# Letting a planner order all five engines of a two-layer diffusion block

## The chip, the cores and the metric

The kernel runs on one core of a Trainium2 chip. A core has five engines that work side by side, each through its own instructions in its own fixed order: TensorE (PE, the matmuls), VectorE (DVE), ScalarE (ACT), GpSimd (POOL) and SyncE (SP, which issues most of the DMAs). An instruction whose input is not there yet holds up everything behind it on its engine. The metric is the device time of one execution in microseconds (us).

## The reference

Two layers work on 256 tokens and 256 context positions of 1024 channels, all in float32. A layer is a half-step FFN, a mixer over four groups of 256 channels, and a second half-step FFN; each is modulated by vectors that a large matrix `ada_w` makes out of a condition vector:

```python
def half_ffn(h, shift, scale, gate, g, wi, wo):
    return h + 0.5 * gate * swiglu(modulate(rms_norm(h, g), shift, scale), wi, wo)
def swiglu(h, wi, wo):
    a, g = jnp.split(h @ wi, 2, axis=-1)       # 1024 -> 2 x 2816
    return (jax.nn.silu(g) * a) @ wo           # 2816 -> 1024
def modulate(h, shift, scale):
    return h * (1 + scale) + shift
```

The mixer's four groups are a pooling, a long convolution with a filter made by a small MLP (hyena), a gated linear attention (GLA) in two directions, and a short convolution. Layer 1's second FFN and the output are needed for the 256 tokens alone.

## The kernel before

**Work.** All activations lie with channels on the 128 partitions and the 512 positions (tokens v = 0, context v = 1) along the free axis. A float32 product is made of three fp32r matmuls (`mm3`, lines 178 to 180): each operand is split into a rounded high part and a low part (`split`: ACT casts `whi`, line 166; DVE subtracts to get `wlo`, line 167). So each weight tile is loaded by DMA (`raw`, 1 MB), cast, subtracted, and multiplied. An up block f of an FFN is 48 matmuls of 128x512 (8 k, two halves, 3 each), and its result goes through Silu (`sg`, lines 500 and 501) and a split (`hh`, `hl`). 22 up blocks and two sweeps of down blocks make an FFN.

**Fp32 matmuls.** Some products stay plain fp32: the statistics of the norm (line 390), the broadcast of their reciprocal root (line 227, `diag`), the modulation vectors of the start (`gemv`, line 280), and the small products of the mixer. The `gemv` ones use a quarter of the array each: `c32` has 32 columns, and step k writes partitions 32(k mod 4) on:

```python
for k in ks:
    g = slice(32 * (k % 4), 32 * (k % 4) + 32)
    self.nc.tensor.matmul(ps[g, :], lhsT=self.c32[:, k, :], rhs=ws[k], start=k < 4, stop=k >= KT - 4)
```

**Modulation.** The other modulation vectors are made on DVE: `acc` (lines 316 and 318) multiplies and adds 128x512 pieces of `ada_w`; transposes (322) and sums (324) follow. This work is cut into small steps by a generator, and `fill` hands out some steps after each FFN block.

**Order.** The framework's scheduler sets the order by priorities in program order. Three tools bend it: `prio` shifts a priority, `mark` and `after` hold an instruction behind one issued earlier, and `start()`, the first two up blocks with the first norm and four slabs of modulation, is issued by hand in written order on PE, DVE and ACT. Its slabs are written as: slab 0 (`part(0)`), first matmuls (lines 1315 to 1318), slab 1, more matmuls, slab 2, and so on, each slab with its 8 `gemv` matmuls in one go. The norm at the start is: squares on ACT (376), sums on DVE (380), line 390 on PE, a chain of 12 small DVE operations (`rsqrt_cols`, 205 to 215), `diag` (225), line 227; then `ny` (421) on DVE, `yh` (428) on ACT, `yl` (429) on DVE.

**GLA.** The mixer computes the logarithm of a decay for both directions (matmul 1080, then ACT: 1082, 1083, a table load, 1086), a scan on DVE (1095), `kexp` (DVE 1106, ACT exponential 1107, DVE 1109), a transposition on PE (1113), and then the states (1151).

## Time and profile before

| | us |
|---|---|
| three runs | 1703.17, 1704.85, 1704.58; median 1704.58 |
| profiled execution | 1703.05 |
| its span, first to last instruction | 1701.3 |
| PE busy | 1672.0 (98%) |
| DVE busy | 1199.1 (70%) |
| ACT busy | 577.8 (34%) |

The stages in the profiled execution, by the first matmul of each: start to 21.1, layer 0 FFN 1 to 408, mixer to 616, FFN 2 to 984, layer 1 FFN 1 to 1358, mixer to 1493, FFN 2 to 1691, output to 1701. A row of a timeline gives the start, the length of the record and the instruction; the records of neighbouring matmuls overlap, so what one costs is the distance from its start to the next one's.

### The profile page before, as it was taken

The page shows a single profiled execution, that of the slowest core. Times are in us where ns is not written, and L with a number is a line of the kernel's source. Part 1 is how long each engine was busy: PE and PEld are TensorE (multiplying, and loading weights), DVE is VectorE, ACT ScalarE, POOL GpSimd, SP SyncE. Part 2 cuts the span into 40 slices and gives each one's busy share as a digit, 9 for nine tenths or more (in the row PEclk, how much of TensorE's full clock was granted, in tenths as well). Part 3 has the DMA queues.
Part 4 walks back from the last instruction along what each step waited for, and adds up shares of the span by engine and source line. Part 5 has one row for each costly group of instructions (what it writes and reads, how often), then busy time and mean ns, then how long its engine had stood idle before and what let it go on. Part 6 is the DMA issues. An engine that isn't in the chain of part 4 may idle for free.

```text
span 1701.3 us, 23406 instructions
## 1 busy us (share of the span) xinstructions
PE 1672.0 (98%) x9590; PEld 1434.0 (84%) x9590; DVE 1199.1 (70%) x2053; ACT 577.8 (34%) x741; POOL 33.6 (2%) x59
## 2 busy tenths in 40 slices
PE   8999999999999999999999999999999998999998
PEld 6888887878888898888888898888878897899998
DVE  5889957896675679888669775654464668875455
ACT  3322213333632443221122242221233354554343
POOL 0000000010000000000000000000000000000010
PEclk9999999999999999999999999999999999999999
DMA  8655544432322325545435425543433234345552
GB/s 331 244 180 190 196 163 164 162 123 98 115 100 93 115 94 184 193 164 176 180 131 203 162 108 176 173 161 137 158 117 118 78 127 161 117 153 174 181 194 78
DMA packets 50875, 262.54 MB, mean 154 GB/s; under 512 B 5946, under 2 KB 10880, under 8 KB 28240
## 3 DMA queue, kind: packets, MB, share of 16 engines
q1 hardware_dynamic: 48672, 255.99, 43.0%
q0 software_dynamic: 1376, 4.00, 0.6%
q8 instruction: 75, 1.23, 0.3%
q10 hardware_dynamic: 720, 1.06, 0.2%
q14 instruction: 32, 0.26, 0.0%
HBM read 257.88 MB, written 3.15 MB: 153 GB/s over the span
## 4 chain that ended last, share of the span: by engine, by line
PE 91%; DVE 5%; ACT 2%; DMA 1%; issue 1%; POOL 0%; DVEq 0%; ACTq 0%; POOLq 0%; SPq 0%
PE psm L178 28%; PE psm L179 27%; PE psm L180 27%; DVE wlo L167 1%; ACT whi L166 1%; DVE acc L318 1%; PE psa L991 1%; PE psm L1315 1%; PE psa L227 1%; DMA x<-in_xt_dram 0%; PE psa L1050 0%; PE psm L1316 0%; PE psa L1228 0%; PE psm L1318 0%; PE psa L390 0%
## 5 line engine op out<-in xcount | busy, mean ns | idle before, releaser
L178 PE MATMUL psm<-yh,whi 128*128 128x512 f32 (+1 forms) x1584 | 555.7, 354 | 4.8 <-ACT yh L428 1.8
L180 PE MATMUL psm<-yh,wlo 128*128 128x512 f32 (+1 forms) x1584 | 556.8, 353 | 2.4 <-DVE wlo L167 2.4
L179 PE MATMUL psm<-yl,whi 128*128 128x512 f32 (+1 forms) x1584 | 556.7, 353 | 0.2 <-DVE yl L429 0.2
L166 ACT CAST whi<-raw 128x2048 fp32r<-128x2048 f32 (+5 forms) x176 | 304.8, 1734 | 596.2 <-PE psm L179 522.2
L167 DVE TENSOR_TENSOR wlo<-raw,whi 128x2048 fp32r<-128x2048 f32 (+5 forms) x176 | 364.3, 2071 | 139.3 <-ACT whi L166 138.9
L178 PEld LDWEIGHTS psm<-yh,whi 128*128 128x128 f32 x1584 | 297.4, 189 | 49.1 <-ACT yh L428 2.3
L180 PEld LDWEIGHTS psm<-yh,wlo 128*128 128x128 f32 x1584 | 299.3, 189 | 44.8 <-DVE wlo L167 3.4
L179 PEld LDWEIGHTS psm<-yl,whi 128*128 128x128 f32 x1584 | 298.9, 189 | 41.2 <-DVE yl L429 0.9
L318 DVE SCALAR_TENSOR_TENSOR acc<-adaw,cvec,acc 128x512 f32<-128x512 f32 x392 | 274.5, 746 | 2.8
L178 PE MATMUL psm<-hh,whi 128*128 128x512 f32 (+1 forms) x752 | 264.7, 352 | 0.0
L180 PE MATMUL psm<-hh,wlo 128*128 128x512 f32 (+1 forms) x752 | 264.6, 352 | 0.0
L179 PE MATMUL psm<-hl,whi 128*128 128x512 f32 (+1 forms) x752 | 264.4, 352 | 0.0
L180 PEld LDWEIGHTS psm<-hh,wlo 128*128 128x128 f32 x752 | 142.3, 189 | 19.3 <-DVE acc L318 0.8
L179 PEld LDWEIGHTS psm<-hl,whi 128*128 128x128 f32 x752 | 142.3, 189 | 19.3 <-DVE hl L167 0.4
L178 PEld LDWEIGHTS psm<-hh,whi 128*128 128x128 f32 x752 | 142.2, 189 | 18.9 <-issue 0.2
L501 DVE TENSOR_TENSOR sg<-psm,sg 128x512 f32<-128x512 f32 (+1 forms) x90 | 54.4, 605 | 127.0 <-PE psm L180 119.8
L484 DVE SCALAR_TENSOR_TENSOR x<-psm,gt,x 128x256 f32<-128x256 f32 x112 | 50.4, 478 | 116.2 <-PE psm L180 116.1
L500 ACT ACTIVATE sg<-psm 128x512 f32<-128x512 f32 (+1 forms) x90 | 47.9, 532 | 208.1 <-PE psm L180 203.6
L376 ACT ACTIVATE sq<-x 128x512 f32<-128x512 f32 (+1 forms) x64 | 32.7, 522 | 91.1 <-DVE x L484 75.1
L178 PE MATMUL psm<-whi,yh 128*128 128x256 f32 (+1 forms) x200 | 58.2, 293 | 1.6 <-ACT whi L166 1.6
L179 PE MATMUL psm<-wlo,yh 128*128 128x256 f32 (+1 forms) x200 | 57.4, 293 | 1.2 <-DVE wlo L167 1.2
L180 PE MATMUL psm<-whi,yl 128*128 128x256 f32 (+1 forms) x200 | 58.0, 290 | 0.0
(291 smaller groups left out, 1515.7 us busy)
## 6 DMA issues: line engine op xcount, KB each, us to landing
raw<-in_ffn_wi_dram SPq DMA_DIRECT2D x86, 1024.0 KB, 4.8
adaw<-in_ada_w_dram SPq DMA_DIRECT2D x68, 1024.0 KB, 5.1
raw<-in_ffn_wo_dram SPq DMA_DIRECT2D x32, 896.0 KB, 4.6
raw<-in_ffn_wo_dram SPq DMA_DIRECT2D x16, 1024.0 KB, 5.0
raw<-in_w_in_dram SPq DMA_DIRECT2D x14, 1024.0 KB, 4.7
raw<-in_w_out_dram SPq DMA_DIRECT2D x8, 1024.0 KB, 4.7
adaw<-in_ada_w_dram SPq DMA_DIRECT2D x16, 256.0 KB, 5.7
pm<-in_k_pool_dram SPq DMA_DIRECT2D x12, 256.0 KB, 2.8
```

The lines of the kernel that those rows point to most:

```text
L166: self.nc.scalar.copy(hi[:, s], src[:, s])
L167: self.nc.vector.tensor_tensor(lo[:, s], src[:, s], hi[:, s].bitcast(F32), op=ALU.subtract)
L178: mm(ps, lhsT=ah, rhs=bh, start=first, stop=False)
L179: mm(ps, lhsT=ah, rhs=bl, start=False, stop=False)
L180: mm(ps, lhsT=al, rhs=bh, start=False, stop=last)
L227: nc.tensor.matmul(ps[:, j * P:(j + 1) * P], lhsT=self.ones, rhs=dg[:, j, :], start=True, stop=True)
L318: nc.vector.scalar_tensor_tensor(acc, ws[half][:, k, :], sc, acc, op0=ALU.mult, op1=ALU.add)
L376: nc.scalar.activation(sq, self.x[m][:, lo:lo + n], AF.Square)
L484: nc.vector.scalar_tensor_tensor(self.x[m][:, s], ps[:, v * S - lo:v * S - lo + S], gate[v][:, m:m + 1], self.x[m][:, s], op0=ALU.mult, op ...
L500: nc.scalar.activation(sg, w[2][:, s], AF.Silu)
L501: nc.vector.tensor_tensor(sg, w[3][:, s], sg, op=ALU.mult)
L991: nc.tensor.matmul(ps[par], lhsT=fwd[:, 2 * i + par, :], rhs=cur[par], start=True, stop=True)
```

## The change

Every call that the builder makes on an engine is written down instead of issued (`_Engine`, `Plan.add`), with what it must follow: earlier calls that touch the same part of the same tile, and, for a tile from a rotating pool, the end of the tile whose place it takes. `cost` gives each call a length. `forward` is a list schedule: the engine that can start first takes the ready call of the lowest rank. `backward` gives latest times. Ten mixtures of early and late times, in two rounds, are tried; the shortest plan is issued in order of its start times, on all five engines. `prio`, `mark` and `after` do nothing any more. The calls themselves are the same.

```diff
+class Plan:
+    def cost(self, eng, op, out, args, kw):
+        if op == "dma_start":
+            return 0.45, 0.0
+        n = self.free(out)
+        if eng == "PE":
+            if op == "transpose":
+                return 0.115, 0.33
+            lhs = kw["lhsT"]
+            m, k = self.free(lhs), lhs.shape[0]
+            if "32r" in str(lhs.dtype):
+                d = max(0.0135 + n / 2400.0, 0.06)
+            else:
+                d = 2 * max(0.112 * min(m, 128) / 128.0, 0.002 + n / 1200.0)
+                if m in (32, 64):
+                    d *= m / 128.0
+                elif k <= 64:
+                    d *= 0.62
+            return d, d + 0.3
+        psum = any(str(a.space).endswith("PSUM") for a in self.aps(args, kw))
+        if eng == "DVE":
+            cyc = {"tensor_tensor_scan": 2.0, "reciprocal": 4.0}.get(op, 1.0)
+            if op == "tensor_reduce":
+                n = self.free(args[1])
+            d = (0.13 if psum else 0.07) + cyc * n / 960.0
+            return d, d + 0.2
+        if eng == "ACT":
+            d = 0.19 + n * 0.8e-3
+            return d, d + 0.2
...
+    def forward(self, rank, queue):
...
+            t, e = best
+            while soon[e] and soon[e][0][0] <= t + 1e-9:
+                r, i = heapq.heappop(soon[e])
+                heapq.heappush(now[e], (rank[i], i))
+            if e == "ACT":
+                _, i = min(now[e], key=lambda x: (x[0] + (2.0 if self.table[x[1]] not in (-1, table) else 0.0), x[1]))
...
+            if e == "ACT" and self.table[i] not in (-1, table):
+                t += 1.3
+                table = self.table[i]
+            start[i] = t
+            order.append(i)
+            clock[e] = t + self.occ[i]
+            if self.bytes[i]:
+                wire = max(wire, t + self.occ[i] + 1.3) + self.bytes[i] / 0.38e6
...
+    def issue(self, tc, rounds=2):
...
+        for _ in range(rounds):
+            start, end = best
+            late = self.backward(start)
+            for early in (start, [i * end / n for i in range(n)]):
+                for share in (0.125, 0.25, 0.375, 0.5, 0.75):
+                    rank = [share * e + (1 - share) * (b + end) for e, b in zip(early, late)]
+                    got = self.forward(rank, self.queue)
+                    if got and got[1] < best[1]:
+                        best = got
+        start = best[0]
+        self.planned = best
+        with tc.manual_schedule():
+            for i in sorted(range(n), key=lambda i: (start[i], i)):
+                fn, args, kw = self.calls[i]
+                fn(*args, **kw)
...
-        self.tc, self.nc, self.t, self.out = tc, tc.nc, t, out
+        self.tc, self.nc, self.t, self.out = tc, Plan(tc.nc), t, out
...
-        with self.tc.manual_schedule(engines={et.PE, et.DVE, et.Activation}):
+        if True:
...
-        Builder(ctx, tc, t, out).run()
+        b = Builder(ctx, tc, t, out)
+        b.run()
+        b.nc.issue(tc)
```

Three places of the new order follow. In it every instruction has the line of the issuing loop (L341), so the names tell them apart; their numbers differ between the two programs.

**ACT at the start.** `x_...` are the eight tiles of the input, `craw` the condition vector, from which Silu makes `cvec`; `sq` are the squares. Before:

```order
L1266 DMA craw_111<-in_cvec_dram 128x16
L370 DMA x_113<-in_xt_dram 128x512
L370 DMA x_115<-in_xt_dram 128x512
L370 DMA x_117<-in_xt_dram 128x512
L370 DMA x_119<-in_xt_dram 128x512
L247 ACT_TABLE_LOAD
L247 ACTIVATE cvec_108<-craw_111 128x16
L376 ACTIVATE sq_228<-x_112 128x512
L376 ACTIVATE sq_230<-x_113 128x512
```

And now, from the fourth `x` on:

```order
L341 DMA x_116<-in_xt_dram 128x512
L341 DMA craw_108<-in_cvec_dram 128x16
L341 ACT_TABLE_LOAD
L341 ACTIVATE sq_146<-x_110 128x512
...
L341 ACTIVATE sq_149<-x_113 128x512
L341 ACTIVATE sq_152<-x_116 128x512
L341 ACT_TABLE_LOAD
L341 ACTIVATE cvec_105<-craw_108 128x16
L341 ACTIVATE sq_151<-x_115 128x512
```

The condition vector is fetched last instead of first, and the Silu with a table load of its own stands between the seventh and the eighth square.

**PE at the start.** `adaw` with `c` is a slab's matmul (line 280); `mean` with `sq` is line 390, `diag` line 227, `psm` the up blocks. Before:

```order
L390 MATMUL psa_251<-mean_102,sq_228 128x2 x4
L280 MATMUL psa_305<-adaw_131,c_41_184 32x512 x4
L280 MATMUL psa_305<-adaw_133,c_41_184 32x512 x4
L227 MATMUL psa_316<-diag_317,ones_100 128x128 x2
L227 MATMUL psa_322<-diag_323,ones_100 128x128 x2
L292 MATMUL psa_330<-sum_22_137,row_314 128x2 x4
L1315 MATMUL psm_295<-yh_277,whi_293 128x512
```

And now, up to the first up matmul, and a piece from slab 3:

```order
L341 MATMUL psa_153<-mean_101,sq_145 128x2 x3
L341 MATMUL psa_191<-adaw_119,c_41_141 32x512 x4
L341 MATMUL psa_191<-adaw_120,c_41_141 32x512 x2
L341 MATMUL psa_153<-mean_101,sq_145 128x2
L341 MATMUL psa_191<-adaw_120,c_41_141 32x512 x2
...
L341 MATMUL psa_202<-adaw_128,c_41_141 32x512
L341 MATMUL psm_181<-yh_163,whi_179 128x512
...
L341 MATMUL psa_212<-adaw_140,c_41_141 32x512
L341 MATMUL psm_181<-yh_165,whi_179 128x512
L341 MATMUL psa_212<-adaw_140,c_41_141 32x512
```

One of the four statistics matmuls stands behind six slab matmuls, six of slab 1's stand ahead of the first up matmul, and the last four of slab 3's stand alone between up matmuls.

**PE in layer 1's GLA.** `kexp` is line 1113, `v` with `kdt` line 1151, `psm` are projections. Before, the two transpositions stand 55 rows apart:

```order
L1113 MATMUL psa_11209<-ident_99,kexp_11205 128x128 x4
L180 MATMUL psm_11443<-whi_11358,yl_10713 128x256
...
L180 MATMUL psm_11524<-yh_10707,wlo_11490 128x256
L1113 MATMUL psa_11233<-ident_99,kexp_11229 128x128 x4
L1151 MATMUL psa_11253<-v_10950,kdt_11214 32x64 x4
```

And now:

```order
L341 MATMUL psm_1964<-whi_1957,yl_1822 128x256
L341 MATMUL psa_1909<-ident_99,kexp_1908 128x128 x4
L341 MATMUL psm_1965<-whi_1960,yh_1807 128x256
L341 MATMUL psa_1916<-ident_99,kexp_1915 128x128 x4
L341 MATMUL psm_1967<-whi_1957,yh_1807 128x256
L341 MATMUL psa_1922<-v_1872,kdt_1910 32x64 x4
```

They are one matmul apart, and the states begin one matmul later.

## Rows read from the trace of the kernel before

**Rows 1.** The page: busy time of each engine; the chain that ended last.

```profile
PE 1672.0 (98%) x9590; PEld 1434.0 (84%) x9590; DVE 1199.1 (70%) x2053; ACT 577.8 (34%) x741; POOL 33.6 (2%) x59
PE 91%; DVE 5%; ACT 2%; DMA 1%; issue 1%; POOL 0%; DVEq 0%; ACTq 0%; POOLq 0%; SPq 0%
```

**Rows 2.** Busy time in stretches: PE, PEld, DVE, ACT, POOL; granted clock; DMA share, GB/s.

```profile
10.00:22.00 12.00, 7.84 (x61) 5.97 (x61) 8.02 (x31) 3.58 (x8) 0.00 (x0) 0.90 1.03 390
22.00:56.00 34.00, 33.62 (x171) 23.22 (x170) 18.40 (x48) 14.49 (x27) 0.00 (x0) 0.93 0.81 309
56.00:400.00 344.00, 342.50 (x1539) 281.63 (x1540) 287.30 (x459) 97.30 (x99) 9.96 (x14) 1.00 0.49 171
100.00:150.00 50.00, 50.00 (x222) 41.40 (x221) 44.43 (x66) 15.03 (x15) 0.00 (x0) 1.00 0.50 172
400.00:425.00 25.00, 21.68 (x162) 19.96 (x161) 19.55 (x62) 10.51 (x24) 1.18 (x3) 1.00 0.20 72
425.00:562.00 137.00, 136.81 (x1026) 113.77 (x1025) 93.09 (x164) 56.07 (x86) 2.10 (x4) 1.00 0.31 106
1355.00:1375.00 20.00, 17.22 (x117) 16.03 (x116) 15.84 (x48) 9.89 (x22) 0.00 (x0) 0.91 0.16 53
1375.00:1493.00 118.00, 110.64 (x967) 100.30 (x966) 94.23 (x205) 62.58 (x108) 1.05 (x2) 1.00 0.41 141
1493.00:1690.00 197.00, 196.28 (x1628) 194.19 (x1627) 111.30 (x138) 84.43 (x98) 7.59 (x8) 1.00 0.47 161
```

**Rows 3.** Timeline of PE at the start: start, length, instruction, idle before.

```profile
13.67 1.02 PE L390 MATMUL psa<-mean,sq 128*128 128x2 f32 x8 [1.56 <-DVE sq L380]
14.63 1.92 PE L280 MATMUL psa<-adaw,c 128*32 128x512 f32 x16
17.25 1.17 PE L227 MATMUL psa<-diag,ones 128*128 128x128 f32 x8 [0.70 <-DVE diag L225]
21.11 0.79 PE L1315 MATMUL psm<-yh,whi 128*128 128x512 f32 x1 [1.91 <-ACT yh L428]
```

**Rows 4.** Timeline of ACT at the start.

```profile
4.04 1.28 ACT L247 ACT_TABLE_LOAD   x1 [4.04 <-DMA craw<-in_cvec_dram]
12.17 0.63 ACT L376 ACTIVATE sq<-x 128x512 f32<-128x512 f32 x1 [2.20 <-DMA x<-in_xt_dram]
```

**Rows 5.** Timeline of PE, eight full-width fp32 matmul records of 512 columns.

```profile
482.29 3.60 PE L991 MATMUL psa<-tok,dft 128*128 128x512 f32 x8
```

**Rows 6.** Groups of DVE instructions, 60 to 350 us: shape, count, busy, mean ns.

```profile
L318 DVE SCALAR_TENSOR_TENSOR acc<-adaw,cvec,acc 128x512 f32<-128x512 f32 x160 | 110.1, 744 | 0.5
L167 DVE TENSOR_TENSOR wlo<-raw,whi 128x2048 fp32r<-128x2048 f32 x18 | 41.2, 2286 | 10.3 <-ACT whi L166 10.3
L322 DVE STREAM_TRANSPOSE acct<-acc 128x256 f32<-128x256 f32 x44 | 16.8, 419 | 0.3
L501 DVE TENSOR_TENSOR sg<-psm,sg 128x512 f32<-128x512 f32 x18 | 12.3, 684 | 7.9 <-PE psm L180 7.9
```

**Rows 7.** Timeline of DVE, a pair of line 318 in one row.

```profile
119.73 1.41 DVE L318 SCALAR_TENSOR_TENSOR acc<-adaw,cvec,acc 128x512 f32<-128x512 f32 x2
```

**Rows 8.** Waits of PE: released by, us in total, times, longest.

```profile
PE psa L227 <- DVE diag L225: 2.2, 5, 0.7
PE psa L1113 <- DVE kexp L1109: 2.1, 2, 1.6
```

**Rows 9.** Timeline of layer 1's GLA: two rows of PE, one of ACT.

```profile
1399.52 0.70 PE L1080 MATMUL psa<-g,gw 96*128 96x512 f32 x2
1411.19 0.66 PE L1113 MATMUL psa<-ident,kexp 128*128 128x128 f32 x4 [1.62 <-DVE kexp L1109]
...
1401.16 1.25 ACT L1082 ACTIVATE la<-psa,vec 128x512 f32<-128x512 f32 x2
```

**Rows 10.** Timeline of PE, a projection matmul and the next state matmul.

```profile
1421.71 0.38 PE L178 MATMUL psm<-yh,whi 128*128 128x256 f32 x1
1422.03 0.70 PE L1151 MATMUL psa<-v,kdt 64*32 64x64 f32 x24
```

More of the change, by code (lines that the diff above doesn't have):

```diff
@@ L1 @@
+import heapq
 import math
@@ L108, in prio @@
     def prio(self, delta):
-        tc = self.tc
-        base = tc.cur_priority
-        tc.cur_priority = max(0, base + delta)
-        start = tc.cur_priority
         yield
-        tc.cur_priority = base + tc.cur_priority - start
     def mark(self, *engines):
-        engines = engines or (mybir.EngineType.DVE, mybir.EngineType.SP)
-        found = {}
-        for i in reversed(self.nc.cur_bb.bb.instructions):
-            if i.engine in engines and i.engine not in found:
-                found[i.engine] = i
-                if len(found) == len(engines):
-                    break
-        return found
+        return None
     @contextmanager
     def after(self, mark):
-        with ExitStack() as es:
-            for i in mark.values():
-                es.enter_context(self.tc.issue_after(i))
-            yield
+        yield
     def consts(self):
@@ L1285, in start @@
         nc.sync.dma_start(out=self.tneg, in_=self.t["k_tneg"])
-        et = mybir.EngineType
         two = [0, 1]
-        with self.tc.manual_schedule(engines={et.PE, et.DVE, et.Activation}):
+        if True:
             self.ada_init(craw)
```

194 lines of the change are left out of this document (added).

## The prediction

> **What bounds the kernel now.** I read the page first. PE is busy 98% of the span and holds 91% of the chain that ended last; DVE is at 70%, ACT at 34% [rows 1]. So an order can win only where PE idles, and it can lose wherever it makes PE's own work longer.
>
> Next the busy time in stretches [rows 2] says where PE idles. From 100 to 150 us it is busy 50.00 of 50 with 222 matmuls, one per 0.225 us: in an FFN there is nothing to win. From 56 to 400 it idles 1.5 of 344 us, from 425 to 562 0.2 of 137, from 1493 to 1690 0.7 of 197. The idle time lies at the start (4.2 of the 12 us from 10 to 22), at the entries of the two mixers (3.3 from 400 to 425, 2.8 from 1355 to 1375) and in layer 1's mixer (7.4 of 118). The granted clock, 1.00 elsewhere, averages 0.90, 0.93 and 0.91 in three of these rows. As its levels are 1.2 and 2.4 GHz, that is 2.4 + 4.8 us at the lower level in the start and 3.6 at the second mixer entry, each time behind a stretch in which PE idled.
>
> Then the timelines of the start [rows 3, 4], of GLA [rows 9] and of a change between matmul forms [rows 10] give the prices.
>
> **Start, step by step.** The planner fetches `craw` last on ACT and puts a table load, 1.28 us [rows 4], ahead of the eighth square, which in the trace starts at 12.17 when its input lands [rows 4]. If the inputs land as late as now, the table load hides in that wait and costs nothing; if not, table load and square push line 390 by up to 1.3 + 0.6 us. I take 0.5, since ACT idled 2.2 us there.
>
> One of the four line-390 matmuls now stands behind six of slab 0's. In the trace line 390 runs at 13.67 and the slab, 1.92 us, at 14.63 [rows 3]. The reciprocal root reads all four columns, so it starts about 1.9 us later. Behind it, `wlo` casts of 512 columns now stand inside the chain on DVE: a cast of 2048 takes 2.29 in the record [rows 6], a quarter of that is 0.6. Before, `yh` was also waited for by PE for 1.91 us at 21.11 [rows 3], so nothing on PE hides this: the sum is 0.5 + 1.9 + 0.6 = 3.0. But before, `ny` also had to wait for the modulation of line 292, which ends behind line 227, so not all of it is new; I take +2.3 (bounds 0.5 and 3.5).
>
> The slabs themselves: 16 records in 1.92 us are two passes of each of 8 matmuls, four column groups side by side, so a round of four takes 0.96 us [rows 3]. A lone one has two passes of 512 columns, and eight such passes took 3.60 us [rows 5], so it takes 0.90, not a quarter of a round. Counted so, slabs 1 to 3 took 6 rounds after the first up matmul. Now slab 1 leaves 2 there (its six stand ahead, in time in which PE waits anyhow), slab 2 takes 2, and slab 3, split 2, 2, 1, 1, 1, 1, takes 6: 10 rounds, +4 x 0.9 = 3.6 us. If a lone matmul cost only an eighth of a slab, 0.24, the term would be 18 x 0.24 less 24 x 0.24 = -1.4; I take 3.6, the nearer row. Nothing hides it: from 22 to 56 PE was busy 33.6 of 34 [rows 2]. As the clock's low stretch will hold fewer up matmuls if they start later, I give back 0.5. Start: **+5.4** (0 to +8).
>
> **First FFN.** The order on DVE packs the `acc` work early. Between two `wlo` casts of up blocks there now stand nine operations of line 318. A pair of them takes 1.41, one record 0.744 [rows 6, 7], so the second starts 0.67 after the first. A cast takes 2.29 less the same 0.07, 2.2; `sg` and `hl` 0.6 each, six transposes and sums up to 0.34 each [rows 6]. That is 6.0 + 2.2 + 1.2 and, in some blocks, 2.0: 9.4 to 11.4, where a block of PE has 48 x 0.225 = 10.8 us. It is even on the average, with two `wlo` buffers as cover. I take **+1** (0 to +4). If the cover were gone, every block with sums would cost 0.6.
>
> **Mixer entries.** Between line 390 and line 227 of the context's half the order before has 15 matmuls, now 43, so the wait for `diag`, 2.2 us over five places [rows 8], and for `yh` behind it goes there. The tokens' half has about as few as before. Of 3.3 + 2.8 idle I take half, and half of what the lower clock cost at the second (3.6 us at half speed lose 1.8): -3.0 - 0.9 = **-3.9** (0 to -7.9). The turns between FFNs hold 1.5 and 0.7 us in their rows [rows 2]; I take **-1** for all of them.
>
> **GLA in layer 1.** From line 1080 at 1399.52 to line 1113 at 1411.19 the chain took 11.7 us, with a PE wait of 1.62 in it [rows 9]. Now 72 matmuls of 256 columns lie between; 1628 in 197 us make 0.12 each [rows 2], so 2 x 0.3 + 72 x 0.12 = 9.2 us of cover. The chain gets another table load, 1.28 [rows 4], and begins up to 0.6 earlier on ACT, which was late at 1401.16 [rows 9]: 12.4, so PE waits 3.2. The second transposition comes a matmul later and waits for its own `kexp`, 0.5; the states follow at once and wait for the copy `kdt` on ACT, which stands behind exponentials, 0.8. That is 4.5 against 2.1 for the two waits now [rows 8]: **+2.4** (-1 to +4). The other 5.3 us of idle in this mixer have more filler than before, projection and output groups dealt out one by one; I take **-4** (0 to -5.3).
>
> **Changes of form.** The planner holds a small fp32 matmul to be as cheap anywhere. From a projection matmul at 1421.71 to the state matmul at 1422.03 it took 0.32 instead of 0.12 [rows 10], so such a visit costs 0.2. Counted in the orders, fp32 work visits the fp32r stream 155 times instead of 99: 7 more at the start, 8 in the FFNs, 41 in the mixers, of which about 20 with tiles smaller than the array. I take 20 x 0.2 less 0.5 that falls into waits: **+3.5** (0, if the change hides, to 56 x 0.2 = 11).
>
> Outside these the matmuls and their lengths are the same, and the last stage has the same chain.
>
> **The sum.** 5.4 + 1 - 3.9 - 1 + 2.4 - 4 + 3.5 = +3.4 on the profiled execution's 1703.05 (span 1701.3 and 1.75 around it); the median of the runs is 1.5 above that execution, so 1704.6 + 3.4 = **1708 us**. Under 0.2%, 3.4 us, a measurement of this kernel can hardly tell from no change; the forecast lies on that edge.
>
> **The rivals.**
>
> *Faster: the plan fills the waits.* What speaks for it is that 13.5 us of idle lie in stretches with other matmuls at hand, and that the planner sees all five engines where the old order saw priorities. If 80% of it goes, with the 1.8 of the clock, and start and form changes cost 5 together, the time falls by 10.8 + 1.8 - 5 = 7.6: **1697**. It decides for this if the wait at line 1113 is under 1 us and the first part of the start costs under 3. Against it: its small DVE operations are planned at 0.07 us plus length, and its chains therefore too short. The Trainium skill, Perfetto Trace Analysis, Optimization Strategy, holds that interleaving stretches in which different engines are contended can gain. Here it does not apply between FFN and mixer as long as PE is full in the one [rows 2].
>
> *Slower: DVE becomes the bound of the first FFN.* Blocks of 11.4 against 10.8 us, once the two buffers' lead is used up, give 0.6 in each of some 17 blocks that carry `acc` work: +10 on top of a balance of nothing else changed by much, **1716**. For it: DVE is busy 287 of 344 us there already [rows 2]. Against it: blocks without sums are 9.4. It decides if PE shows waits for `wlo` between 150 and 350 us.
>
> *Slower: every change of form costs.* If all 56 additional visits cost 0.2, not just those with small tiles, the term is 11.2 instead of 3.5: **1716**. For it is the one row of the price [rows 10]; against it, that full-array fp32 matmuls load and stream like the others. The Trainium skill, TensorEngine Tiling (Array Packing), Tiling Modes, says that a change of the tiling mode drains TensorE. By that rule only the visits with small tiles cost, which gives the forecast's term; the 0.2 us of the trace agree with it.
>
> *The change does nothing* can be left out: the order differs on all engines.
>
> **How the numbers follow.** Forecast 0.45, with its own range of 1701 to 1714; filled waits 0.28; DVE bound 0.13; all form changes 0.14. The forecast splits into 0.06 faster, 0.20 the same and 0.19 slower; the filled waits give 0.27 faster and 0.01 the same; of the two slow rivals 0.04 come out the same. So faster 0.33, same 0.25, slower 0.42. The range leaves out 1 in 10 on each side: 1691, where the filled waits meet a start near its lower bound, to 1718, just past the slow rivals.
>
> **What the profile after would show.** First up matmul near 23.4 instead of 21.1, the lone slab matmuls 0.9 apart from what follows, end of the first two blocks some 5 us later; no new PE waits for `wlo` at 100 to 350 us; shorter idle at the mixer entries and no low clock at the second; a wait of about 3 us at line 1113; 0.3 instead of 0.12 around small-tile visits. Wrong would be the forecast if lone slab matmuls take 0.24, if PE's idle time in layer 1's mixer falls under 3 us, or if waits for `wlo` repeat block after block.

## The result, and the profile after

The changed kernel takes 1767.47 us, median of 4 runs (1766.51 to 1770.54), against 1703.88 (1702.84 to 1704.85) for the kernel before on the same chip. The ratio is 1.0376, with a 95% interval of 1.0358 to 1.0394: 64 us slower, where 1708 and at most 1718 had been forecast.

The page of the kernel after: busy time of each engine, the chain that ended last by engine; below them the answer on the core, with the mean granted clock. Every instruction has the line of the issuing loop, so only engines and names speak.

```profile
PE 1708.9 (97%) x9590; PEld 1448.6 (82%) x9590; DVE 1224.7 (69%) x2053; ACT 580.9 (33%) x744; POOL 32.9 (2%) x59
PE 48%; DVE 21%; issue 2%; ACT 1%; DMA 1%; SPq 0%; DVEq 0%; ACTq 0%
...
core 0: 1765.9 us, clock 0.986
```

DVE's part of the chain has gone from 5% to 21% [rows 1], though its busy share is a point lower. These shares add up to 74%: the chain could be followed back to 456 us only, so the first FFN and the first mixer's entry are not in it. The span is 64.6 us longer. PE idles 1765.9 - 1708.9 = 57.0 us instead of 29.3: +27.7. The mean clock was 0.996 before and is 0.986 now, so 0.014 x 1765.9 = 24.7 us of work were lost to the lower level instead of 0.004 x 1701.3 = 6.8: +17.9. The other 19 us PE was busy longer without idling or the lower clock, on the same matmuls.

By stage, each counted from the first statistics matmul of its norm to that of the next stage's:

| stage | before | after | |
|---|---|---|---|
| start and layer 0 FFN 1 | 388.7 | 415.3 | +26.6 (and 1.7 ahead of it) |
| layer 0 mixer | 208.1 | 218.2 | +10.1 |
| layer 0 FFN 2 | 368.1 | 386.7 | +18.6 |
| layer 1 FFN 1 | 374.2 | 376.9 | +2.7 |
| layer 1 mixer | 143.1 | 146.1 | +3.0 |
| layer 1 FFN 2, output | 205.4 | 207.3 | +1.9 |

Which work PE waits for, in the kernel after: released by, us in total, times, longest.

```profile
PE psm L341 <- DVE wlo L341: 16.2, 19, 1.8
PE psa L341 <- DVE sq L341: 5.3, 3, 2.4
PE psa L341 <- DVE kexp L341: 4.7, 1, 4.7
PE psm L341 <- DVE hl L341: 4.6, 2, 2.5
```

And for `wlo` in the kernel before, 3.6 us in all:

```profile
PE psm L180 <- DVE wlo L167: 2.4, 3, 1.1
PE psm L179 <- DVE wlo L167: 1.2, 2, 0.6
```

Busy time in stretches of the kernel after (PE, PEld, DVE, ACT, POOL, granted clock, DMA share, GB/s):

```profile
64.00:300.00 236.00, 222.74 (x950) 180.77 (x950) 228.86 (x350) 54.70 (x52) 4.48 (x6) 0.96 0.54 191
100.00:150.00 50.00, 50.00 (x222) 41.38 (x222) 48.15 (x70) 14.34 (x13) 0.00 (x0) 1.00 0.50 172
200.00:250.00 50.00, 45.62 (x187) 36.61 (x186) 48.67 (x77) 9.80 (x8) 0.00 (x0) 0.93 0.52 179
300.00:430.00 130.00, 129.94 (x601) 106.89 (x599) 69.72 (x100) 45.76 (x52) 4.07 (x6) 1.00 0.28 96
428.00:453.00 25.00, 23.46 (x165) 22.38 (x164) 21.32 (x69) 11.39 (x27) 1.62 (x3) 0.93 0.43 139
750.00:850.00 100.00, 91.21 (x381) 72.70 (x382) 97.37 (x150) 22.79 (x22) 1.07 (x2) 0.97 0.54 186
1414.00:1434.00 20.00, 18.98 (x144) 17.95 (x143) 18.79 (x63) 10.41 (x25) 0.54 (x1) 1.00 0.40 131
1434.00:1558.00 124.00, 116.64 (x976) 104.03 (x975) 95.97 (x204) 65.84 (x111) 1.05 (x2) 0.97 0.38 129
```

The first FFN falls into two halves. Up to 300 us DVE is busy 97% and PE loses; from 300 on DVE is at 54% and PE full. DVE itself waits for almost nothing between 64 and 300 (1.7 us for the casts `whi`): it is the bound there. PE's waits in this stretch are 5.8 us for `wlo` (0.8 of them ahead of 64), 3.3 for `hh` and `hl`, and the two below. The first, put down to "issue", is for the sums `red` of the `acc` work: the last of them ends on DVE at 92.89. The second is for a DMA of the mixer's small MLP and has nothing to do with DVE; another 0.7 is for ACT in the same MLP.

```profile
92.99 1.86 PE L341 MATMUL psa<-red,sel 128*128 128x16 f32 x8 [2.18 <-issue]
287.07 0.44 PE L341 MATMUL psa<-z,hw 33*64 33x128 f32 x4 [2.04 <-DMA hw<-in_hy_mlp_dram]
```

FFN 2 of layer 0 shows the same as the first half from 750 to 850: PE waits 5.2 us for `wlo` and 3.6 for `hh` and `hl`.

One block of DVE's work between 64 and 300, on its timeline, from one `hl` to the next:

```profile
180.01 0.68 DVE L341 TENSOR_TENSOR hl<-sg,hh 128x512 fp32r<-128x512 f32 x1
180.62 0.44 DVE L341 STREAM_TRANSPOSE acct<-acc 128x256 f32<-128x256 f32 x1
181.09 0.42 DVE L341 TENSOR_REDUCE red<-acct 128x8 f32<-128x256 f32 x1
...
182.23 0.48 DVE L341 TENSOR_SCALAR acc<-adaw,cvec 128x512 f32<-128x512 f32 x1
182.74 2.33 DVE L341 SCALAR_TENSOR_TENSOR acc<-adaw,cvec,acc 128x512 f32<-128x512 f32 x3
184.98 0.48 DVE L341 TENSOR_SCALAR acc<-adaw,cvec 128x512 f32<-128x512 f32 x1
185.50 2.33 DVE L341 SCALAR_TENSOR_TENSOR acc<-adaw,cvec,acc 128x512 f32<-128x512 f32 x3
187.74 0.68 DVE L341 TENSOR_TENSOR sg<-psm,sg 128x512 f32<-128x512 f32 x1
188.34 1.53 DVE L341 SCALAR_TENSOR_TENSOR acc<-adaw,cvec,acc 128x512 f32<-128x512 f32 x2
189.79 2.28 DVE L341 TENSOR_TENSOR wlo<-raw,whi 128x2048 fp32r<-128x2048 f32 x1
192.00 0.68 DVE L341 TENSOR_TENSOR hl<-sg,hh 128x512 fp32r<-128x512 f32 x1
```

It takes 11.99 us, where PE's block takes 10.8. By the plan's own `cost` the same operations take 10 x 0.603 (`acc`) + 4 x 0.337 (transposes, sums) + 2.203 (`wlo`) + 0.663 (`sg`) + 0.603 (`hl`) = 10.85: the planner filled DVE to PE's block, by prices 10% too low. The pair at 188.34 has a record of 1.53; that of [rows 7] had 1.41. In the order before, two accumulators mostly took turns; the planner lets the operations on one accumulator follow each other, each reading what the one ahead of it wrote. From the start of one multiply-add to the start of one right behind it the median is 0.787 us, 0.663 in the order before (where 212 of 278 such pairs are at 0.66 and 66 at 0.78).

What this does on PE, at the end of the same block and two blocks on:

```profile
192.13 0.50 PE L341 MATMUL psm<-yh,wlo 128*128 128x512 f32 x1 [0.80 <-DVE wlo L341]
...
213.94 0.50 PE L341 MATMUL psm<-hh,whi 128*128 128x512 f32 x1 [0.82 <-ACT hh L341]
216.96 0.80 PE L341 MATMUL psm<-hl,whi 128*128 128x512 f32 x1 [2.51 <-DVE hl L341]
217.55 0.63 PE L341 MATMUL psm<-hh,wlo 128*128 128x512 f32 x1
```

`wlo` is 0.8 late. Two blocks later PE runs one matmul between waits of 0.82 and 2.51, and then the matmuls start 0.43 apart (0.227 before them), the lower of the clock's two levels, until 222.2. Two more such stretches lie between 64 and 300: from 92.8 to 99.7, from the end of the wait of 2.18 for `red` on, and from 287.4 to 290.8, behind the 2.04 for the DMA. Together they are 17.1 us, and half of that, 8.5, is lost. In FFN 2 the clock falls at 833.5, in a wait of 2.05 for `hl` that stands one matmul behind one of 1.52 for `hh`. The waits for `wlo` in these two stretches are 1.5 us at most each, and no low stretch begins right behind one of them.

### The profile page after: what moved, and what is told of

Same layout as the page of the kernel before. It is cut to its first block, busy times and chain, and to the rows that moved or that the text cites. A ratio compares the mean times of both kernels' runs of the same rounds, so it can differ in the third digit from the quotient of the medians.

```text
span 1765.9 us, 23420 instructions
## 1 busy us (share of the span) xinstructions
PE 1708.9 (97%) x9590; PEld 1448.6 (82%) x9590; DVE 1224.7 (69%) x2053; ACT 580.9 (33%) x744; POOL 32.9 (2%) x59
## 4 chain that ended last, share of the span: by engine, by line
PE 48%; DVE 21%; issue 2%; ACT 1%; DMA 1%; SPq 0%; DVEq 0%; ACTq 0%
PE psm L341 45%; DVE acc L341 7%; DVE wlo L341 4%; PE psa L341 3%; DVE acct L341 1%; DVE red L341 1%; DVE sm L341 1%; DVE yl L341 1%; DVE ny L341 1%; DVE x L341 1%; ACT whi L341 1%; DVE hl L341 1%; DVE sg L341 1%; DVE sq L341 1%; ACT la L341 0%
## 5 line engine op out<-in xcount | busy, mean ns | idle before, releaser
L341 PE MATMUL psm<-yh,wlo 128*128 128x512 f32 (+1 forms) x1616 | 572.9, 356 | 10.4 <-DVE wlo L341 10.3
L341 PE MATMUL psm<-yh,whi 128*128 128x512 f32 (+1 forms) x1616 | 572.3, 358 | 1.8 <-ACT yh L341 1.8
L341 PE MATMUL psm<-yl,whi 128*128 128x512 f32 (+1 forms) x1616 | 570.5, 356 | 0.9 <-DVE yl L341 0.8
L341 ACT CAST whi<-raw 128x2048 fp32r<-128x2048 f32 (+5 forms) x176 | 304.5, 1732 | 547.5 <-PE psm L341 498.9
L341 DVE TENSOR_TENSOR wlo<-raw,whi 128x2048 fp32r<-128x2048 f32 (+5 forms) x176 | 363.8, 2068 | 102.1 <-ACT whi L341 94.4
L341 PEld LDWEIGHTS psm<-yh,wlo 128*128 128x128 f32 x1616 | 307.0, 190 | 60.1 <-DVE wlo L341 15.7
L341 PEld LDWEIGHTS psm<-yh,whi 128*128 128x128 f32 x1616 | 305.5, 191 | 53.0 <-issue 8.0
L341 PEld LDWEIGHTS psm<-yl,whi 128*128 128x128 f32 x1616 | 306.9, 190 | 45.3 <-DVE yl L341 2.3
L341 DVE SCALAR_TENSOR_TENSOR acc<-adaw,cvec,acc 128x512 f32<-128x512 f32 x392 | 292.4, 750 | 11.4 <-DMA adaw<-in_ada_w_dram 1.9
L341 PE MATMUL psm<-hl,whi 128*128 128x512 f32 (+1 forms) x752 | 268.1, 357 | 4.7 <-DVE hl L341 4.6
L341 PE MATMUL psm<-hh,wlo 128*128 128x512 f32 (+1 forms) x752 | 268.8, 358 | 3.6 <-DVE wlo L341 3.6
L341 PE MATMUL psm<-hh,whi 128*128 128x512 f32 (+1 forms) x752 | 267.6, 357 | 2.3 <-ACT hh L341 2.3
L341 DVE TENSOR_TENSOR sg<-psm,sg 128x512 f32<-128x512 f32 (+1 forms) x90 | 54.4, 604 | 232.8 <-PE psm L341 232.0
L341 PEld LDWEIGHTS psm<-hl,whi 128*128 128x128 f32 x752 | 143.9, 191 | 25.7 <-DVE hl L341 6.1
L341 PEld LDWEIGHTS psm<-hh,wlo 128*128 128x128 f32 x752 | 143.8, 191 | 25.0 <-DVE wlo L341 5.5
L341 PEld LDWEIGHTS psm<-hh,whi 128*128 128x128 f32 x752 | 143.8, 191 | 22.3 <-ACT hh L341 3.2
L341 DVE SCALAR_TENSOR_TENSOR x<-psm,gt,x 128x256 f32<-128x256 f32 x112 | 50.3, 479 | 90.1 <-PE psm L341 90.1
L341 ACT ACTIVATE sg<-psm 128x512 f32<-128x512 f32 (+1 forms) x90 | 47.7, 530 | 176.6 <-PE psm L341 176.6
L341 ACT CAST hh<-sg 128x512 fp32r<-128x512 f32 (+1 forms) x90 | 49.5, 550 | 136.1 <-DVE sg L341 136.0
L341 ACT ACTIVATE sq<-x 128x512 f32<-128x512 f32 (+1 forms) x64 | 32.4, 521 | 86.7 <-DVE x L341 77.6
L341 PE MATMUL psm<-wlo,yh 128*128 128x256 f32 (+1 forms) x200 | 58.9, 297 | 1.7 <-DVE wlo L341 1.7
L341 PE MATMUL psm<-whi,yh 128*128 128x256 f32 (+1 forms) x200 | 60.1, 304 | 0.2 <-ACT whi L341 0.2
```

What stands on the lines that cost most here:

```text
L341: fn(*args, **kw)
```

## Experiments

The theory: **DVE's work on `acc` was priced too low for the neighbours that the plan gives it, so the plan filled DVE past what PE's blocks cover, and PE's waits for DVE brought the lower clock with them.** Rivals: the start, the changes of form, or the loss of the holds that spread DVE's work out. All versions but one are made from the kernel after; ratios are to the kernel before, on the same chip.

**1. Neighbours that alternate.** The `acc` steps of all vectors take turns, the transposes come before the sums, and this work keeps that order in the plan.

```diff
+                nc.row = True
+                for k in range(4):
+                    for vi, v in enumerate(vecs):
...
+        if self.row and eng == "DVE":
+            if self.last >= 0:
+                preds[self.last] = True
+            self.last = i
```

> The planned kernel with one constraint more: the accumulation work on DVE (multiply-adds, transposes, sums) keeps one fixed order in which the two vectors' accumulators alternate, and two transposes stand before their two sums. The planner's costs are unchanged. Theory A, neighbours: a multiply-add right behind one on the same accumulator starts 0.79 us after it, one behind another accumulator 0.66, so the planned kernel's DVE work is some 30 us longer per layer-0 FFN than planned and PE waits for wlo. By A the two FFNs of layer 0 lose most of their 20.8 + 18.6 us and the time falls from 1767 to 1730, between 1722 and 1740. Theory B, packing: DVE is filled to 97% early in each FFN, and any full DVE makes PE wait. By B the time stays within 10 us of 1767.

1722.92 us, ratio 1.0115 (1.010 to 1.013): 44.6 us came back. The same stretch, then a piece of it, then two rows of DVE's timeline:

```profile
64.00:300.00 236.00, 236.00 (x1051) 194.14 (x1050) 225.96 (x372) 70.81 (x67) 6.77 (x8) 1.00 0.56 201
200.00:250.00 50.00, 50.00 (x222) 41.40 (x222) 50.00 (x89) 8.51 (x5) 1.06 (x2) 1.00 0.64 228
...
205.24 1.40 DVE L346 SCALAR_TENSOR_TENSOR acc<-adaw,cvec,acc 128x512 f32<-128x512 f32 x2
208.50 6.05 DVE L346 SCALAR_TENSOR_TENSOR acc<-adaw,cvec,acc 128x512 f32<-128x512 f32 x9
```

DVE is fuller than ever, 50.00 of 50, and PE does not miss a cycle: nine operations in 6.05 are 0.66 each. In the 236 us PE does 101 matmuls more than in the kernel after, 101 x 0.225 = 22.7 us, which is close to what that kernel lost there: 13.3 idle and 8.5 by the clock. By stage the profiled execution gains 23.1 us in FFN 1 behind the first two blocks, 16.7 in FFN 2 of layer 0 and 6.1 in the mixer between them. So a full DVE is not what hurts, as long as its operations take about what the plan takes them for; and the lower clock goes with the waits. The 2.7 us of waits in the mixer's MLP are gone as well, so not all of the gain is the neighbours'.

**2. The price alone.** The neighbours stay as planned; only `cost` knows what they take.

```diff
+            name = out.name.split("_")[0]
+            if name in ("acc", "acct", "red"):
+                d = {"acc": 0.79 if op == "scalar_tensor_tensor" else 0.51, "acct": 0.47, "red": 0.34}[name]
```

> The planned kernel with nothing but the price of the accumulation work corrected: 0.79 us for a multiply-add of 512 (planned: 0.60), 0.51 for the first one, 0.47 for a transpose and 0.34 for a sum, as they take in the planned kernel's own trace. No dependency is added, so the neighbours may stay as they are. If the FFNs' loss comes from a plan that fills DVE by a price 20 to 25% too low, it goes though the neighbours stay: near 1725, at least 35 us back. If the neighbours themselves hurt (DVE full of long steps whatever the plan knows), less than 20 us come back: 1748 to 1765.

1735.75 us, ratio 1.0191 (1.0174 to 1.0208): 31.7 us back, between the two expectations. In stretches of FFN 1 and FFN 2, and a row of DVE:

```profile
76.00:92.00 16.00, 9.49 (x33) 7.23 (x31) 15.44 (x24) 1.90 (x1) 0.00 (x0) 0.79 0.54 198
92.00:423.00 331.00, 330.22 (x1495) 271.71 (x1494) 276.77 (x417) 93.15 (x97) 10.09 (x15) 1.00 0.46 163
800.00:850.00 50.00, 50.00 (x223) 41.40 (x222) 47.69 (x72) 10.64 (x7) 1.07 (x2) 1.00 0.56 201
...
806.46 2.99 DVE L344 SCALAR_TENSOR_TENSOR acc<-adaw,cvec,acc 128x512 f32<-128x512 f32 x4
```

The neighbours are still the slow ones (0.75 apart here, median 0.786), but with true prices FFN 2 of layer 0 is back at 370.1 us, and FFN 1 loses nothing after 92 us. What FFN 1 still loses (409.9 with the start) lies before. The first two blocks end at 65.5, later than in the kernel after (62.1); then comes one wait of 6.5 for `wlo`, with the lower clock behind it. Ahead of that `wlo` DVE does `acc` work without a gap from 67.41 to 82.45, 15.0 us against a block's 10.8 on PE, while the cast `whi` for it ended at 79.99: here the plan packs too much in spite of the true price, and why it does was not told apart. So this run gives back FFN 2 but for 2.0 us, and about half of FFN 1.

**3. A price by dependence.** `scalar_tensor_tensor` costs 0.06 more, and a DVE operation that needs the result of an earlier one can start 0.12 after that one's slot; matmul groups of one PSUM tile keep their written order.

```diff
-            d = (0.13 if psum else 0.07) + cyc * n / 960.0
+            d = (0.13 if psum or op == "scalar_tensor_tensor" else 0.07) + cyc * n / 960.0
...
+            return self.occ[i] + (0.12 if self.eng[i] == "DVE" else 0.0)
```

> The planned kernel with two DVE costs corrected: 0.13 instead of 0.07 us of fixed time for three-operand operations, and 0.12 more before a DVE operation may start that depends on an earlier one of DVE; accumulation groups of one PSUM tile also keep their written order. By theory A the planner interleaves by itself and knows how full DVE is, so the FFN losses go and the chains of the norms get cover: 1725, between 1712 and 1738. By theory B about 1750, as DVE is still filled early.

1725.91 us, ratio 1.0128 (1.0112 to 1.0145): 41.6 back. Told of the lag, the planner puts something else in between by itself, and the median between neighbours is 0.663 again. FFN 1 with the start is at 389.8, FFN 2 at 372.4. That is theory A's expectation.

**4. The holds given back.** `mark` and `after` become dependencies of the plan.

```diff
+        if eng in self.hold:
+            preds[self.hold[eng]] = True
```

> The planned kernel with the holds of the kernel before given back as dependencies: an accumulation step may not start ahead of the last DVE and SP call noted before its turn. Neighbours on the same accumulator stay as they are. By theory B (packing early) the waits for wlo go and the time falls to about 1730. By theory A (neighbours) the steps stay long, but DVE needs about 310 of 360 us of an FFN, so spread out they cost some waits only where several fall in one block: 1740 to 1755.

1744.44 us, ratio 1.0241 (1.0226 to 1.0256): 23.0 back, 12.8 of them in FFN 2 and 5.9 in FFN 1 with the start. Spreading the work out helps, with the same slow neighbours (0.787), but less than the price does. Theory A's range held, theory B's 1730 did not.

**5. The slow neighbours in the kernel before.** Its `acc` work is held in written order, everything else is left alone.

```diff
+                def held(fn, *args, **kw):
+                    with ExitStack() as es:
+                        if self.prev is not None:
+                            es.enter_context(self.tc.issue_after(self.prev))
+                        fn(*args, **kw)
+                    self.prev = self.mark(mybir.EngineType.DVE)[mybir.EngineType.DVE]
```

> The kernel before, in the framework's order and with its pacing, with one thing changed: each accumulation step is held behind the one written before it, so that the four multiply-adds on one accumulator follow each other and each sum follows its transpose, as the planner ordered them. Theory A (neighbours): DVE takes some 2.6 us more per slab, 31 us per layer-0 FFN, of which DVE's idle time there (about 40 us of 246) takes most: 5 to 20 us slower than 1703.4. Theory B (packing): no packing here, so within 3 us of 1703.4.

1704.89 us, ratio 1.0015 (1.0005 to 1.0024). In stretches and on DVE's timeline:

```profile
56.00:402.00 346.00, 343.17 (x1529) 281.28 (x1528) 299.06 (x457) 98.75 (x101) 10.02 (x14) 1.00 0.48 168
...
125.30 1.53 DVE L315 SCALAR_TENSOR_TENSOR acc<-adaw,cvec,acc 128x512 f32<-128x512 f32 x2
```

DVE is 11 us busier than in the kernel before (287.93 in the same stretch) and PE hardly notices. Theory A's 5 to 20 us did not come; the 2.1 lie in theory B's range. Slow neighbours alone do little where DVE has idle time to take them. So neither a full DVE (experiment 1) nor slow neighbours by themselves make the loss: it takes both, slow neighbours at the wrong price on a DVE that the plan has filled.

**6, 7. The start.** First every engine keeps the written order of the start, and `craw` is loaded first.

```diff
+        if self.line is not None:
+            if eng in self.line:
+                preds[self.line[eng]] = True
+            self.line[eng] = i
```

> The planned kernel with the first two blocks, the first norm and the four modulation slabs kept in their written order on every engine, and the condition vector fetched first. Both theories of the FFNs: the first up matmul goes back from 25.8 to about 21, the lone slab matmuls are gone, and the start gives back its 7.6 us: 1760, between 1756 and 1764. If the start's loss is hidden by what DVE does behind it (theory A or B with DVE as the bound of the whole stage), less than 3 us come back.

1804.28 us, ratio 1.0595 (1.0576 to 1.0614): a miss. With PE held to an order the planner put later loads of `ada_w` ahead of the slabs, and PE waited:

```profile
PE psa L346 <- DMA adaw<-in_ada_w_dram: 28.8, 5, 8.8
```

Then the same with the later DMAs behind the start's last one, on top of experiment 1:

```diff
+        if dma and self.first:
+            preds[self.first[-1]] = True
```

> The planned kernel with alternating accumulators, and the start in its written order on every engine with the condition vector fetched first; no DMA of later work may be issued ahead of the start's last one. In the run with the start's order alone later loads had been planned ahead of the slabs, and PE waited 28.8 us for them; with that excluded the start should cost what it does in the kernel before: first up matmul near 21, first statistics of the mixer near 402, total 1722.9 less 3.5 to 6, so 1717 to 1720. If the later stages depend on what the planner could load early, the FFN takes it back and the time stays at 1723.

1716.04 us, ratio 1.0082 (1.0067 to 1.0097), 6.9 less than experiment 1. The first up matmul starts at 20.5 instead of 27.7, and the first two blocks end at 52.8 instead of 60.4: of these 7.6 us 6.9 reach the total. Experiment 1's start is not the kernel after's, where the two times are 25.8 and 62.1, but its blocks end nearly as late. So the start is worth about 7 us, and what follows doesn't hide it.

**8. Changes of form.** Experiment 3 with a planner that, on PE, prefers a matmul of the same form by 1.5 us of rank and charges 0.13 for a change.

```diff
+                pick = min(near, key=lambda x: (x[0] + (1.5 if self.form[x[1]] != form else 0.0), x[1]))
...
+                if self.form[i] != form:
+                    t += 0.13
```

> The planned kernel with the corrected DVE costs, and with a liking for one form of matmul: among the ready PE calls one whose form (small tiles or not) differs from the last one's counts 1.5 us later, and a change is charged 0.13 us. If visits of small-tile matmuls cost 0.27 us each, as the distances in the traces say, and their number falls from 46 to about 30, the time falls by 3 to 5 us from 1725.9, to 1721 or 1723; the lone slab matmuls join too and give another 2. If the visits cost nothing that is on the path, it stays within 2 us of 1725.9.

1717.36 us, ratio 1.009 (1.0075 to 1.0105): 8.6 less than experiment 3, with 37 small-tile visits instead of 46. Nine visits at the 0.27 us estimated below are 2.4; the rest came with an order that moved everywhere, so this run sizes nothing.

**9 to 12. Together.** All of 1, 3, 7 and 8 in one:

> All corrections at once on the planned kernel: alternating accumulators, corrected DVE costs, the start in written order, the liking for one form. If the losses are separate and add up, 1767.5 less 44.6 for the neighbours, less 5 for the start, less 4 for the form: 1714, between 1706 and 1720. It beats the kernel before, 1703.4, only if the corrected costs also fill the waits of the mixers.

1715.01 us, ratio 1.0071 (1.0051 to 1.0091): no better than 7 alone; its four runs spread from 1709.4 to 1717.5. In the profiled execution, 1709.4, most of the loss lies at turns between stages: around two of them (605 to 630, 975 to 1000) PE is busy 21.4 and 21.0 of 25 us at a clock of 0.80 and 0.86, where the kernel before has 24.0 and 24.2 at 1.00. Here is the chain of small DVE operations from the statistics to `diag`, at the turn from FFN 2 of layer 0 to layer 1:

```profile
980.69 0.15 DVE L380 TENSOR_SCALAR sm<-psa 128x2 int32<-128x2 int32 x1
...
980.95 0.74 DVE L380 SCALAR_TENSOR_TENSOR acc<-adaw,cvec,acc 128x512 f32<-128x512 f32 x1
...
986.78 0.47 DVE L380 TENSOR_SCALAR diag<-ident,sm 128x128 f32<-128x128 f32 x2
```

6.1 us, where the kernel before took 2.4 for it (979.21 to 981.63). The lag of 0.12 made the planner see gaps between operations of two columns, and it put larger ones into them, multiply-adds of 0.66 and a cast of 1.1 among them. Two ways out were tried. PE in written order at the turns:

```diff
+        if self.pe and eng == "PE":
+            if self.pe_last >= 0:
+                preds[self.pe_last] = True
+            self.pe_last = i
```

> The version with all corrections (1715.0), and PE kept in its written order from the last output blocks of an FFN or mixer to the end of the first two blocks of the next FFN, since that version's trace lost some 16 us at three such turns, in waits and in the lower clock behind them. If the loss there is the planner's order on PE, the turns go back to the length they have in the kernel before and the time falls by 8 to 14 us, to 1701 or 1707. If it comes from DVE and ACT, whose order there is still planned, it stays above 1711.

1728.34 us, ratio 1.0144 (1.0129 to 1.0159): a miss, 13 more; PE now waits 12.9 us for `diag`, in five places. And a true price for tiny operations, without a lag:

```diff
+        self.tiny.append(eng == "DVE" and self.free(out) <= 4)
+        if self.tiny[-1]:
+            occ, vis = 0.195, 0.395
```

> The version with all corrections (1715.0, without the written order at the turns), and one cost more: the small operations of the reciprocal root's chain (up to four columns) are charged as 0.195 us of DVE's own time each instead of 0.07 and a gap of 0.12. In the trace of that version the planner filled those gaps with multiply-adds of 0.66 us, and the chain took 6 us from statistics to diag instead of 2.4. If this stretched chain is what the turns lose by, they get some 2 us each and part of the lower clock back: 1715 less 6 to 12, so 1703 to 1709. If the turns lose by what stands ahead of the chain (the last output blocks, sums), it stays within 3 us of 1715.

1708.37 us, ratio 1.0038 (1.0027 to 1.0049): 6.6 less than without (its seven runs spread from 1706.0 to 1713.3), and the chain:

```profile
985.26 0.15 DVE L384 TENSOR_SCALAR sm<-psa 128x2 int32<-128x2 int32 x1
...
988.22 0.28 DVE L384 TENSOR_SCALAR diag<-ident,sm 128x128 f32<-128x128 f32 x1
```

3.0 us. That the shorter chains brought all of the 6.6 is not shown: the execution profiled here is one of 1713.3, slower than the one with the chain of 6.1. Last, the holds of experiment 4 on top:

> The same as the run on the chain, and the holds of the kernel before as dependencies, so that accumulation work can't move ahead into the turns and mixers. If accumulation work at the turns is what is left of the loss, a further 2 to 5 us: 1700 to 1706, as good as the kernel before or better. If the holds cost more than they give (in the pair of runs without the other corrections they left the first FFN longer), it is slower than the run on the chain by 3 to 10 us.

1705.86 us, ratio 1.0017 (1.0007 to 1.0026). No version is faster than the kernel before; this one is 0.2% slower, by an interval that just leaves out no change.

## Why the prediction was wrong, step by step

**First FFN, +1: the step that failed.** The range's upper end fell with it. Measured is +20.7 behind the first two blocks, and +18.6 in FFN 2 of layer 0, for which the sum had no term. The step took 0.67 for a multiply-add from a pair of the order before [rows 7], where the neighbour works on another accumulator, and found blocks of 9.4 to 11.4 "even on the average". In the new order the neighbour is usually the same accumulator's, 0.787 (some 220 of 238 times), a transpose and its sum go from 0.343 and 0.298 to 0.471 and 0.336, and the block shown is 11.99. With these times the step's own sum gives 10.5 to 12.9 instead of 9.4 to 11.4, which is not even. PE is full from 100 to 150 us (50.00 of 50), right behind a wait and a stretch at the lower clock, and no longer from 200 to 250 (45.62); how much the two `wlo` buffers covered is not shown. Experiments 1 and 2 show this cause from both sides, by making the neighbours fast or the price true, the second for FFN 2 nearly whole and for FFN 1 by half. And 2.7 of waiting and 1.7 by the clock in FFN 1 belong to the mixer's small MLP, which the plan had put there and the step did not look at.

The rival "DVE becomes the bound of the first FFN" had the mechanism and the sign by which it decides (waits for `wlo` between 150 and 350 us), but 0.6 a block; the excess of the block shown is 1.2, and the clock, which this rival had not counted, took 8.5 us beside 13.3 of waiting from 64 to 300. FFN 1 lost 20.7 us instead of 10, and FFN 2 of layer 0, which it did not name, 18.6 more. (Its total does not add up either: 1704.6 + 10 is 1715, not 1716.)

The Trainium skill, VectorE: DVE Perf Modes, The DRAIN you can't avoid, has the next DVE operation wait until the pipe is empty, with or without a semaphore between the two, and adds that an operation that is not held starts earlier. By the wait alone the same operation would take one time whatever it reads; the rows here have two, 0.663 and 0.787, and the measurement decides. Whether the shorter one is the section's operation that is not held, no run here shows.

**Start, +5.4.** Measured +7.6: the first two blocks end at 62.1 instead of 54.5, and experiment 7 gives 6.9 back. Rows of PE and two of ACT:

```profile
15.39 0.83 PE L341 MATMUL psa<-mean,sq 128*128 128x2 f32 x6 [2.40 <-DVE sq L341]
...
23.48 2.43 PE L341 MATMUL psa<-adaw,c 128*32 128x512 f32 x12
25.84 0.50 PE L341 MATMUL psm<-yh,whi 128*128 128x512 f32 x1
26.96 1.05 PE L341 MATMUL psa<-adaw,c 128*32 128x512 f32 x2
27.93 0.73 PE L341 MATMUL psm<-yl,whi 128*128 128x512 f32 x2
...
13.27 0.61 ACT L341 ACTIVATE sq<-x 128x512 f32<-128x512 f32 x1
24.10 1.31 ACT L341 ACTIVATE yh<-ny,mods 128x256 fp32r<-128x256 f32 x3 [0.28 <-DVE ny L341]
```

The first up matmul is at 25.84, 4.7 later (2.3 forecast, 3.5 the bound). The 0.5 for the table load was too little: that square starts at 13.27 instead of 12.17, PE waits 2.40 for the squares' sums, and the statistics run 1.7 later. And slab 1's six matmuls do not stand "in time in which PE waits anyhow": all of `yh` for the first up matmul was there by 25.4 at the latest (the row at 24.10), by 24.6 if it needed two pieces as before, while PE worked on the slab without a gap from 23.48 to 25.84. So these matmuls held it up by 0.4 to 1.2 us, for which the step had no term. The lone slab matmul was right: 26.96 to 27.93 is 0.97 (0.90 forecast).

**Mixer entries, -3.9.** Right: the idle time went from 3.3 to 1.5 and from 2.8 to 1.0, and the second entry has its clock, 1.00 instead of 0.91; but the first lost its own, 0.93 instead of 1.00. Together about -3.5, but that is luck in part, as the first entry's clock had no term. The mixer of layer 0 is 10.1 longer all the same; 6.1 of that went away with experiment 1; there is `acc` work in it as well, and from 550 to 650 us DVE is busy 98.06 of 100.

**GLA, +2.4, and the other waits of that mixer, -4.** Three rows, one of PE and two of ACT:

```profile
1465.14 1.11 PE L341 MATMUL psa<-ident,kexp 128*128 128x128 f32 x4 [4.71 <-DVE kexp L341]
...
1459.60 1.89 ACT L341 CAST whi<-raw 128x2048 fp32r<-128x2048 f32 x1
1461.50 1.28 ACT L341 ACT_TABLE_LOAD   x1
```

The wait is 4.7 instead of 2.1, so +2.6, though by another way than forecast: one wait, not three, because a cast of 1.89 as well as the table load stands ahead of the exponential. Behind the entry the mixer idles 7.4 us as before; without `kexp` that is 2.7 instead of 5.3, so -2.6. Its clock is 0.97 now (one stretch of 6.8 us at the lower level), which costs 3.4 and had no term.

**Changes of form, +3.5.** The step had the right kind, with too few and too cheap. In the trace there are 57 visits to small tiles instead of 30; going in, one costs about 0.1 (in the median the small matmul starts 0.21 instead of 0.12 behind a matmul of 256 columns, 0.33 instead of 0.23 behind one of 512); coming out, an estimated 0.13 to 0.17. With 0.27 for both, 27 x 0.27 = 7.3, an estimate. Visits to full-array fp32 matmuls cost about nothing (0.121 instead of 0.120 going in behind 256 columns); so the third rival is out. The rule of the Trainium skill that the prediction quoted (TensorEngine Tiling (Array Packing), Tiling Modes) agrees.

**Turns, -1.** It did not come: the FFN stages of layer 1 are 2.7 and 1.9 longer, and in experiment 9 a turn's chain was lengthened by the plan. How much of the kernel after's loss lies at turns was not told apart.

Of the 19 us that PE was busy longer at its full clock, form changes make an estimated 7.3 and four more rounds of lone slab matmuls 3.9; the other 8 were not assigned, and their cause stays open.

## What to carry to other kernels

A duration that is read from a trace holds for the neighbours it had there: before it goes into a sum or a planner, look whether the new order makes the operation read the result of the one just ahead. A plan that fills an engine off the bottleneck to the length of the bottleneck's block by its own prices (10.85 us for 10.8) has no tolerance: 10% of error in them went to the bottleneck block after block, and the clock took more than half of that again; where DVE has slack, the same neighbours cost 2 us (experiment 5). A static order needs either prices that are measured in its own kind of neighbourhood, or slack on the engine that feeds the bottleneck.

## What was not expected of the hardware

A DVE operation that reads its predecessor's result starts 0.12 to 0.13 us later than one that doesn't: 0.787 against 0.663 for 512 columns of multiply-add, 0.471 against 0.343 for a transpose of 256 with its sum behind it; whether a wait on the result or the pipe makes it, the trace does not show. And the lower clock came back with single waits of 2.18 and 2.04 us, and in the second of two waits of 0.82 and 2.51 us with one matmul between them; in the whole run it cost 24.7 us, 17.9 more than before.
